# A two-layer diffusion trunk: layer 0's experts in 12 groups instead of 13, gathered and scattered two groups at a time, its branch after the first group, and a ring of 12 weight places

## The chip, the cores and the metric

The kernel runs on one core of one Trainium2 chip, as one program. The metric is the device time of one execution in microseconds. Of the kernel before there are three runs, with a median of 1575.86 us (1575.17 to 1578.94). One more execution was taken with the hardware profiler; every row quoted below comes from that one.

## The reference

256 latent tokens and 256 context tokens of width 1024 go through two layers. A layer is a mixer (layer 0: convolution and differential attention; layer 1: gated linear attention) and then a mixture of 32 experts, of which every token picks two inside one group of eight. Layer 0's experts see all 512 tokens, layer 1's only the 256 latent ones. All weights are 32-bit floats.

```python
def hier_moe(xt, rg_w, rg_b, re_w, re_b, w1, w3, w2):
    lg = (xt @ rg_w).astype(jnp.float32) + rg_b
    pg = jax.nn.softmax(lg, axis=-1)
    _, gi = lax.top_k(lg, 1)
    ...
    top_v, top_i = lax.top_k(le_sel, TOP_K)
    gate = pg_sel * jax.nn.softmax(top_v, axis=-1)
    expert = gi * EXPERTS_PER_GROUP + top_i
    ...
    def expert_block(args):
        xb, e = args
        h = jax.nn.silu(xb @ w1[e]) * (xb @ w3[e])
        return h @ w2[e]
    y_rows = lax.map(expert_block, (x_rows, blk_exp)).reshape(n_row, d)
    y = jax.ops.segment_sum(y_rows * row_gate[:, None].astype(y_rows.dtype), row_tok,
                            num_segments=n_tok + 1)
    return y[:n_tok]
```

W1 and W3 of an expert are 1024 x 512, W2 is 512 x 1024, so that an expert has 6 MB of weights and a layer 192 MB. On the inputs that the reference draws, the experts 0 to 3 of layer 0 get 24, 22, 15 and 17 tokens, the largest of the others 67, and no expert of layer 1 more than 28 (counted by computing the routing of the reference).

## The kernel before

**Weights.** All large weights are read as tiles of 128 x 2048 floats (1024 KB each), issued by SyncE (SP), into a ring of places. An expert is six such tiles, two each of W1, W3 and W2; a layer's experts are 192. Four places are a tile pool with four rotating buffers that lives for the whole kernel (`wt`); others are opened per layer where memory is free by then (`wx`, and in layer 1 a few that reuse other buffers, such as `H`). `wtile` walks round the ring with the counter `ring_at`. In layer 0 the ring has 14 places: four of the base, nine by `LATE`, one by `more`. SP issues in program order, and a load whose place isn't free holds up every later one.

**Groups.** The tokens of an expert are placed in slots, and a group of experts has 128 slots: `PAIR` is two experts with 64 slots each, `MIX` three with 64, 32 and 32, `QUAD` four with 32. Layer 0 has 13 groups, (PAIR, PAIR, (96, 32), MIX, PAIR, MIX, ...), layer 1 has eight QUADs. The first four experts (`E0`) are taken as they are, the others sorted on the chip by their counts, so that full experts meet wide slots; SP then has to read the sorted expert numbers (`numi`, line 1494) into registers before it can issue their loads.

**What a group does.** `group_hot` makes the one-hot matrix P, tokens by slots. `gather` multiplies it with the modulated tokens X, held in two parts XH + XL for precision: 16 matmuls of 128 x 512 (line 1386) put the slots' rows into PSUM, ScalarE and VectorE copy them, and eight transposes (line 1400) turn them into `xgT`. `gates` (line 1431) and `slots_T` (line 1411) make the gates `gc` and the transposed P, `G`. `up` (line 1526) multiplies with W1 and W3, `act_h` makes the gated h and transposes it (line 1443), `down` (line 1535) multiplies with W2, `split_y` splits the result in two parts. `scatter` (line 1463) multiplies with G and adds to the residual H: per 128 tokens two PSUM banks with two matmuls each, then a multiplication on VectorE (line 1467) and an addition, half of it on VectorE and half on GpSimd (line 1468). The gather of the next group and the scatter of the last stand between up and down of the present one.

**The branch.** Tokens that find no slot are handled by `rest`: every engine reads a count (`nri`) and branches over a loop that takes one expert per turn, with six tiles of the ring. In layer 0 it stands after group 3 (`REST`), behind a `scatter` of that group. The loop's six tiles count in `ring_at` although no turn runs: 102 + 271 + 11 loads of expert tiles are in the profile, which is 2 x 192.

**Before the experts.** Layer 0's routing is a long chain on VectorE. `modulate` makes XL for 128 tokens at a time (line 1230), alternately on GpSimd and VectorE; `crowded` sorts the experts. The first 14 tiles are loaded ahead of the routing's end.

## Time and profile before

| what | us |
| --- | --- |
| median of three runs | 1575.86 |
| profiled execution | 1574.82 |
| its span in the trace | 1573.1 |
| PE busy in the span | 1331.3 |
| VectorE busy | 674.0 |
| layer 0's experts, first up matmul to last down matmul | 354.79 to 859.66 |
| layer 0's last addition to H ends | 875.66 |

The profile lists, for every engine, when it was busy and what ended the idle time before an instruction. PE is TensorE, PEld its loading of stationary operands, DVE VectorE, ACT ScalarE, POOL GpSimd, SP SyncE; an engine's name with a q behind it is the engine's instruction stream (issues, branches). A 32-bit float matmul is recorded twice. "DMA share" is the busy share of the core's 16 DMA engines, and GB/s what they moved; "PEclk" is the granted TensorE clock as a share of full speed. L12 is line 12 of the kernel.

### The profile page before, as it was taken

The page shows a single profiled execution, that of the slowest core. Times are in us where ns is not written, and L with a number is a line of the kernel's source. Part 1 is how long each engine was busy: PE and PEld are TensorE (multiplying, and loading weights), DVE is VectorE, ACT ScalarE, POOL GpSimd, SP SyncE. Part 2 cuts the span into 40 slices and gives each one's busy share as a digit, 9 for nine tenths or more (in the row PEclk, how much of TensorE's full clock was granted, in tenths as well). Part 3 has the DMA queues.
Part 4 walks back from the last instruction along what each step waited for, and adds up shares of the span by engine and source line. Part 5 has one row for each costly group of instructions (what it writes and reads, how often), then busy time and mean ns, then how long its engine had stood idle before and what let it go on. Part 6 is the DMA issues. An engine that isn't in the chain of part 4 may idle for free. (4 is left out here: it accounts for less than half of the span.)

```text
span 1573.1 us, 19365 instructions
## 1 busy us (share of the span) xinstructions
PE 1331.3 (85%) x7541; PEld 671.3 (43%) x7541; DVE 674.0 (43%) x1301; ACT 369.0 (23%) x706; POOL 338.7 (22%) x234
## 2 busy tenths in 40 slices
PE   5998989859997999999998799988776678778776
PEld 4765647643443434343332487776322122212211
DVE  4589885762245133334334838676202012102121
ACT  3255554531010100001001366444100000000000
POOL 1477402430012011111012545462000000000000
PEclk9999978889997999999999799999798899999998
DMA  9867162377995799999998824468599999999995
GB/s 315 297 222 256 53 215 58 102 299 295 400 376 213 324 422 423 422 423 422 422 404 293 319 88 161 164 216 321 236 426 426 427 427 427 427 427 426 427 427 240
DMA packets 100829, 498.11 MB, mean 317 GB/s; under 512 B 17605, under 2 KB 30248, under 8 KB 45948
## 3 DMA queue, kind: packets, MB, share of 16 engines
q1 hardware_dynamic: 96780, 490.37, 77.9%
q0 software_dynamic: 1680, 6.16, 1.2%
q8 instruction: 61, 1.00, 0.2%
q10 hardware_dynamic: 2272, 0.28, 0.1%
q14 instruction: 36, 0.29, 0.1%
HBM read 495.68 MB, written 1.10 MB: 316 GB/s over the span
## 5 line engine op out<-in xcount | busy, mean ns | idle before, releaser
L1526 PE MATMUL pj<-wx,xgT 128*32 128x512 f32 (+1 forms) x1616 | 330.9, 639 | 59.7 <-DMA wx<-in_moe_w_dram 56.7
L1468 POOL TENSOR_TENSOR H<-H,sc 128x512 f32<-128x512 f32 x68 | 86.7, 1275 | 899.1 <-DVE sc L1467 899.1
L1535 PE MATMUL pj<-wx,hT 128*32 128x512 f32 (+1 forms) x824 | 184.7, 608 | 5.0 <-ACT hT L1445 2.8
L1440 DVE SCALAR_TENSOR_TENSOR s<-s,gc,pj 128x512 f32<-128x512 f32 x21 | 15.7, 747 | 399.6 <-PE pj L1526 328.4
L1526 PEld LDWEIGHTS pj<-wx,xgT 128*32 128x32 f32 (+1 forms) x1616 | 79.8, 120 | 249.0 <-issue 137.8
L1526 PE MATMUL pj<-wt,xgT 128*32 128x512 f32 (+1 forms) x648 | 151.5, 603 | 18.4 <-DMA wt<-in_moe_w_dram 17.7
L370 POOL TENSOR_TENSOR wl<-wt,wh 128x1024 fp32r<-128x1024 f32 x50 | 126.8, 2543 | 144.0 <-ACT wh L369 135.4
L289 PE MATMUL pj<-wh,XH 128*128 128x512 f32 x304 | 123.7, 418 | 15.2 <-ACT p L621 6.8
L290 PE MATMUL pj<-wl,XH 128*128 128x512 f32 x304 | 124.2, 409 | 1.6 <-POOL wl L370 1.6
L1467 DVE TENSOR_TENSOR sc<-wk,g 128x512 f32<-128x512 f32 x136 | 87.6, 686 | 85.5 <-PE wk L1463 83.7
L291 PE MATMUL pj<-wh,XL 128*128 128x512 f32 x304 | 123.6, 408 | 0.2
L1535 PEld LDWEIGHTS pj<-wx,hT 128*32 128x32 f32 (+1 forms) x824 | 44.1, 115 | 94.1 <-issue 81.6
L369 ACT ACTIVATE wh<-wt 128x1024 fp32r<-128x1024 f32 x66 | 69.3, 1056 | 54.4 <-PE pj L291 35.4
L1468 DVE TENSOR_TENSOR H<-H,sc 128x512 f32<-128x512 f32 x68 | 79.6, 1171 | 2.0
L289 PEld LDWEIGHTS pj<-wh,XH 128*128 128x128 f32 x304 | 59.0, 195 | 44.1 <-issue 10.1
L1526 PEld LDWEIGHTS pj<-wt,xgT 128*32 128x32 f32 (+1 forms) x648 | 38.6, 117 | 90.4 <-issue 56.9
L1439 ACT ACTIVATE s<-pj 128x512 f32<-128x512 f32 x21 | 12.5, 597 | 252.4 <-PE pj L1526 245.2
L543 DVE SCALAR_TENSOR_TENSOR wk<-hp,vt,wk 128x512 f32<-128x512 f32 x90 | 67.6, 751 | 1.7
L290 PEld LDWEIGHTS pj<-wl,XH 128*128 128x128 f32 x304 | 59.4, 195 | 16.4 <-POOL wl L370 2.7
L291 PEld LDWEIGHTS pj<-wh,XL 128*128 128x128 f32 x304 | 59.3, 195 | 15.4 <-DVE XL L1094 1.2
L1535 PE MATMUL pj<-wt,hT 128*32 128x512 f32 (+1 forms) x280 | 62.0, 599 | 2.4 <-ACT hT L1445 2.4
L1445 ACT ACTIVATE hT<-trps 128x512 f32<-128x512 f32 x21 | 12.5, 597 | 215.2 <-PE trps L1443 215.2
(461 smaller groups left out, 1982.0 us busy)
## 6 DMA issues: line engine op xcount, KB each, us to landing
wx<-in_moe_w_dram SPq DMA_DIRECT2D x271, 1024.0 KB, 18.6
wt<-in_moe_w_dram SPq DMA_DIRECT2D x102, 1024.0 KB, 19.4
wa<-in_ada_w_dram SPq DMA_DIRECT2D x16, 1024.0 KB, 5.7
wt<-in_gla_w_in_dram SPq DMA_DIRECT2D x12, 1024.0 KB, 6.9
H<-in_moe_w_dram SPq DMA_DIRECT2D x11, 1024.0 KB, 19.6
S<-in_ada_w_dram SPq DMA_DIRECT2D x10, 1024.0 KB, 5.2
wt<-in_ada_w_dram SPq DMA_DIRECT2D x8, 1024.0 KB, 5.3
wt<-in_ab_w_in_dram SPq DMA_DIRECT2D x6, 1024.0 KB, 10.7
```

The costliest lines, as they stand in the source:

```text
L289: nc.tensor.matmul(ps, sh, mh, start=k0, stop=False)
L290: nc.tensor.matmul(ps, sh, ml, start=False, stop=False)
L291: nc.tensor.matmul(ps, sl, mh, start=False, stop=k1)
L369: nc.scalar.activation(wh, w, AF.Copy)
L370: (nc.vector if dve or alt and q % 2 else nc.gpsimd).tensor_sub(wl, w, wh.bitcast(FT))
L543: e.scalar_tensor_tensor(av, hp[:, cb, :, t:t + 256], cw[:, t, cb:cb + 1], av, op0=OP.mult, op1=OP.add)
L1439: nc.scalar.activation(s, h1, AF.Silu)
L1440: nc.vector.scalar_tensor_tensor(s, s, gc, h3, op0=OP.mult, op1=OP.mult)
L1467: nc.vector.tensor_mul(t, ps[:, c], g2[:, b // 2, c])
L1468: (nc.vector if hf else nc.gpsimd).tensor_add(H[:, b, c], H[:, b, c], t)
L1526: nc.tensor.matmul(ps[o:o + w], xgT[:, k, o:o + w], W[nm, x, k // 4][:, k % 4], start=k == 0, stop=k == 7)
L1535: nc.tensor.matmul(ys[hf][o:o + w], hT[:, k, o:o + w], W["2", x, k // 2][:, k % 2, hf * 512:(hf + 1) * 512], start=k == 0, stop=k == 3)
```

## The change

Layer 0 has 12 groups: the first four experts are one QUAD, and (96, 32), MIX, PAIR, MIX, ... follow. They are handled in pairs, (0, 1), (2, 3) to (10, 11). Layer 1 keeps its groups and its functions.

- `gather0` takes the place of `gather` in layer 0. The tokens X are now the stationary operand and P, 256 slots wide for both groups of a pair, is the moving one; the product is `xgT` itself, so that there are no transposes, and ScalarE copies it out of PSUM. It takes 64 matmuls, 256 columns wide for a pair and 128 wide for the groups 0 and 1, which are gathered singly.
- `scatter0` sums both groups of a pair in one PSUM bank (four matmuls), so that the multiplication and the additions on VectorE and GpSimd run once for two groups. It stands after the up of the next pair's first group.
- `rest` comes after the down of group 0, without a scatter ahead of it, and sets `ring_at` back behind it. Group 1's one-hot matrix, gather and gates come behind `rest`.
- The ring has 12 places (`LATE` 7 for 9), and its four base places have tags of their own instead of a rotating pool; the mixers use them too, so that some loads there take another place.
- `crowded` comes before the first gather; XL is made on GpSimd alone; the loads of a group are asked for at other steps (`i in (2, 4)`).

On the TensorE at layer 0's branch, the program of before ended the pre-branch part with group 3's scatter; these are the last rows ahead of the branch and the branch itself:

```order
L1463 MATMUL wk<-yh,G 128x512 x2
L1463 MATMUL wk<-yl,G 128x512 x2
L1680 TENSOR_LOAD nri
L1681 COMPARE_AND_BRANCH
L1682 TENSOR_LOAD nri
L1683 COMPARE_AND_BRANCH
```

In the changed program the rows at that place are group 0's up, the transposes of h, and its down:

```order
L1547 MATMUL pj<-wx,xgT 32x512 x24
L1547 MATMUL pj<-wt,xgT 32x512 x16
L1450 MATMUL trps<-cst,s 128x128 x4
L1556 MATMUL pj<-wx,hT 32x512 x32
L1701 TENSOR_LOAD nri
L1703 COMPARE_AND_BRANCH
```

The scatter left this place: group 0's part of it now runs with group 1's, inside and behind group 2's up, and the branch is three groups earlier.

On SP's queue, the last rows ahead of the branch before the change are loads for group 4, each behind a wait (ISA) for its place:

```order
L1483 DMA wt<-in_moe_w_dram 128x2048
L1483 ISA
L1483 DMA wx<-in_moe_w_dram 128x2048
L1483 ISA
L1483 DMA wx<-in_moe_w_dram 128x2048
L1681 COMPARE_AND_BRANCH
```

In the changed program the last four loads ahead of the branch are group 1's W1, in the base places; behind them SP reads nine expert numbers and then branches. The rows from the last two of these loads on:

```order
L1503 DMA wt<-in_moe_w_dram 128x2048
L1503 ISA
L1503 DMA wt<-in_moe_w_dram 128x2048
L1514 TENSOR_LOAD numi
L1514 ISA x2
```

So 28 tiles are issued ahead of the branch, of which group 0 uses 24; group 1's other eight come right behind it.

On the TensorE inside a pair, around a group's down, before:

```order
L1535 MATMUL pj<-wx,hT 32x512 x17
L1400 MATMUL trps<-cst,xg 128x128 x4
L1431 MATMUL trps<-tab,P 128x2 x4
L1463 MATMUL wk<-yh,G 128x512 x2
L1463 MATMUL wk<-yl,G 128x512 x2
L1535 MATMUL pj<-wx,hT 32x512 x12
L1411 MATMUL trps<-identr,P 128x128 x4
```

The changed program around the down of group 3 (wt, hT), ahead of which the second half of the next pair's gather (L1382) has just ended:

```order
L1438 MATMUL trps<-tab,P 128x3 x3
L1484 MATMUL wk<-yha,G 128x512
L1484 MATMUL wk<-yla,G 128x512
L1417 MATMUL trps<-identr,P 128x128 x4
L1556 MATMUL pj<-wt,hT 64x512 x8
L1484 MATMUL wk<-yhb,G 128x512
L1484 MATMUL wk<-ylb,G 128x512
```

The transposes of L1400 are gone, and the scatter of a pair opens its banks with the first group's parts (yha, yla), while the second group's (yhb, ylb) follow behind its down.

The diff, cut to its core:

```diff
-TURN = (120, 1)
-LATE = (9, 11)
+LATE = (7, 11)
...
-GROUPS = ((PAIR, PAIR, (96, 32), MIX, PAIR, MIX, PAIR, MIX, PAIR, MIX, PAIR, MIX, MIX), (QUAD,) * 8)
-REST = (3, 1)
+GROUPS = ((QUAD, (96, 32), MIX, PAIR, MIX, PAIR, MIX, PAIR, MIX, PAIR, MIX, MIX), (QUAD,) * 8)
+REST = (0, 1)
...
         if not late:
-            return ring.tile([128, 2048], FT, name="wt", tag="wt")
-        f = late[(ring_at[0] + TURN[1] * (ring_of[1] == "ring0" and ring_at[0] >= TURN[0])) % len(late)]
+            base_at[0] += 1
+            return base(base_at[0] - 1)
         ring_at[0] += 1
-        return f()
+        return late[(ring_at[0] - 1) % len(late)]()
+
+    def base(i):
+        return ring.tile([128, 2048], FT, name="wt", tag=f"wt{i % RING}")
...
-            (nc.gpsimd if last and b % 2 == 0 else nc.vector).tensor_sub(X[1][:, :, t], xv, X[0][:, :, t].bitcast(FT))
+            (nc.gpsimd if last else nc.vector).tensor_sub(X[1][:, :, t], xv, X[0][:, :, t].bitcast(FT))
...
+                def gather0(P, dst):
+                    n = P.shape[-1]
+                    m = min(8, 512 // n)
+                    for k0 in range(0, 8, m):
+                        ps = wk()[:, 0:m * n].rearrange("p (k s) -> p k s", k=m)
+                        for k in range(m):
+                            for b in range(nb):
+                                for h in range(2):
+                                    nc.tensor.matmul(ps[:, k], M['X'][h][:, k0 + k, b * 128:(b + 1) * 128], P[:, b],
+                                                     start=b == 0 and h == 0, stop=b == nb - 1 and h == 1)
+                        nc.scalar.activation(dst[:, k0:k0 + m], ps, AF.Copy)
...
+                def scatter0(Gs, ys):
+                    for b in range(nb):
+                        for hf in range(2):
+                            ps = wk()
+                            n = 2 * len(Gs)
+                            for i in range(n):
+                                nc.tensor.matmul(ps, Gs[i // 2][:, b * 128:(b + 1) * 128], ys[i // 2][i % 2][:, hf], start=i == 0, stop=i == n - 1)
+                            c = slice(512 * hf, 512 * hf + 512)
+                            t = ep.tile([128, 512], FT, name="sc", tag="sc", bufs=2)
+                            nc.vector.tensor_mul(t, ps, g2[:, b // 2, c])
+                            (nc.vector if hf else nc.gpsimd).tensor_add(H[:, b, c], H[:, b, c], t)
...
                     for i, _ in enumerate(zip(*es_)):
-                        if i in (0, 4):
+                        if i in (2, 4):
                             yield W
...
                     n = nc.values_load(nri[0:1, 0:1], min_val=0, max_val=64)
+                    at = ring_at[0]
                     with tc.If(n > 0):
...
+                    if l == 0:
+                        ring_at[0] = at
...
-                    if j == REST[l] and l == 0:
-                        scatter(*prev)
-                        prev = None
-                        rest()
...
+                    for j in range(0, NG, 2):
+                        ys = []
+                        nxt = None
+                        for i in range(2):
+                            g = groups[j + i]
+                            hs = up(W, xgT[:, :, ab[i]], g)
+                            for _ in ld:
+                                pass
+                            hT = act_h(hs[0], hs[1], gc[i])
+                            W2 = W
+                            if i == 0 and prev is not None:
+                                scatter0(*prev)
+                            if j + i + 1 < NG:
+                                ld = load_group(groups[j + i + 1])
+                            if i and j + 2 < NG:
+                                P = frtile([nb, 256], "P", 1)
+                                for x in range(2):
+                                    group_hot(groups[j + 2 + x], P=P[:, :, ab[x]])
+                                nxt = pair_tiles()
+                                gather0(P, nxt[0])
+                                gcn = [prep0(x, groups[j + 2 + x], nxt[1]) for x in range(2)]
+                            y = down(W2, hT, g)
+                            ys.append(split_y(y, "ab"[i]))
+                            if j + i + 1 < NG:
+                                W = next(ld)
+                                if j + i == REST[l]:
+                                    rest()
+                                    P = frtile([nb, 256], "P", 1)
+                                    group_hot(groups[1], P=P[:, :, ab[1]])
+                                    gather0(P[:, :, ab[1]], xgT[:, :, ab[1]])
+                                    gc[1] = prep0(1, groups[1], G)
+                                W = next(ld)
+                        prev = ([G[:, x] for x in range(2)], ys)
+                        if nxt:
+                            (xgT, G), gc = nxt, gcn
+                    scatter0(*prev)
```

More of the change, by code (lines that the diff above doesn't have):

```diff
@@ L113, in wtile @@
         if not late:
-            return ring.tile([128, 2048], FT, name="wt", tag="wt")
-        f = late[(ring_at[0] + TURN[1] * (ring_of[1] == "ring0" and ring_at[0] >= TURN[0])) % len(late)]
+            base_at[0] += 1
+            return base(base_at[0] - 1)
         ring_at[0] += 1
-        return f()
+        return late[(ring_at[0] - 1) % len(late)]()
+    def base(i):
+        return ring.tile([128, 2048], FT, name="wt", tag=f"wt{i % RING}")
     def open_ring(es, name, side, n, more=(), order=None):
-        f = [lambda: ring.tile([128, 2048], FT, name="wt", tag="wt")] * RING
+        f = [lambda i=i: base(i) for i in range(base_at[0], base_at[0] + RING)]
         for i in range(n):
@@ L1726, in moe, with pair_tiles, prep0 @@
-                scatter(*prev)
+                            if l:
+                                scatter(pre[1], split_y(ov_down(W, hT2)))
+                            else:
+                                scatter0([pre[1]], [split_y(ov_down(W, hT2), "b")])
+                    if l == 0:
+                        ring_at[0] = at
+                NG = len(groups)
+                if l == 0:
+                    P = frtile([nb, 256], "P", 1)
+                    ab = [slice(0, 128), slice(128, 256)]
+                    def pair_tiles():
+                        return (ep.tile([128, 8, 256], FT, name="xgT", tag="xgT", bufs=1),
+                                frtile([2, nb * 128], "G", 2))
+                    def prep0(i, g, G):
+                        gc = gates(P[:, :, ab[i]], g)
+                        slots_T(P[:, :, ab[i]], G=G[:, i])
+                        return gc
+                    group_hot(groups[0], pos0, P[:, :, ab[0]])
+                    crowded()
+                    xgT, G = pair_tiles()
+                    gather0(P[:, :, ab[0]], xgT[:, :, ab[0]])
+                    gc = [prep0(0, groups[0], G), None]
+                    prev = None
+                    ld = load_group(groups[0])
+                    for _ in range(2):
+                        W = next(ld)
[26 more added lines that the diff above has]
+                                    rest()
+                                    P = frtile([nb, 256], "P", 1)
+                                    group_hot(groups[1], P=P[:, :, ab[1]])
+                                    gather0(P[:, :, ab[1]], xgT[:, :, ab[1]])
+                                    gc[1] = prep0(1, groups[1], G)
+                                W = next(ld)
+                        prev = ([G[:, x] for x in range(2)], ys)
+                        if nxt:
+                            (xgT, G), gc = nxt, gcn
+                    scatter0(*prev)
+                else:
+                    P0 = group_hot(groups[0], pos0)
+                    crowded()
+                    pr = prep(groups[0], P0)
+                    nG = slots_T(pr[1])
+                    prev = None
+                    ld = load_group(groups[0])
+                    for _ in range(2):
+                        W = next(ld)
+                    for j, g in enumerate(groups):
+                        xgT, P, gc = pr
+                        G = nG
+                        hs = up(W, xgT, g)
+                        for _ in ld:
+                            pass
+                        hT = act_h(hs[0], hs[1], gc)
+                        W2 = W
+                        if j + 1 < NG:
+                            ld = load_group(groups[j + 1])
+                        if j + 1 < NG:
+                            pr = prep(groups[j + 1], group_hot(groups[j + 1]))
+                        if prev is not None:
+                            scatter(*prev)
+                        if j + 1 < NG:
+                            nG = slots_T(pr[1])
+                        if j == REST[l]:
+                            rest()
+                        ys = down(W2, hT, g)
+                        if j + 1 < NG:
+                            for _ in range(2):
+                                W = next(ld)
+                        prev = (G, split_y(ys))
+                    scatter(*prev)
```

85 lines of the change are left out of this document (24 added, 61 removed).

## The prediction

> **What bounds the kernel now.** I read the page's slices first, then a table of windows over layer 0's experts, then the timeline around the place where the table shows a hole. In the page's slices (DMA's busy tenths, and what the DMA engines moved; a slice is 39 us) both expert stages stand out at 422 to 427 GB/s, with one low slice in the first of them, the thirteenth:
>
> ```profile
> DMA  9867162377995799999998824468599999999995
> GB/s 315 297 222 256 53 215 58 102 299 295 400 376 213 324 422 423 422 423 422 422 404 293 319 88 161 164 216 321 236 426 426 427 427 427 427 427 426 427 427 240
> ```
>
> The windows (PE, PEld, DVE, ACT and POOL busy with counts, then granted clock, DMA share, GB/s) show the stage itself and its losses:
>
> ```profile
> 350.00:360.00 10.00, 8.63 (x40) 4.10 (x39) 0.69 (x1) 1.19 (x2) 0.00 (x0) 0.97 0.07 14
> 360.00:370.00 10.00, 10.00 (x51) 4.17 (x50) 1.29 (x4) 1.88 (x2) 0.00 (x0) 1.00 0.99 397
> 380.00:390.00 10.00, 10.00 (x47) 3.61 (x48) 2.01 (x3) 2.39 (x4) 0.00 (x0) 1.00 0.63 238
> 450.00:460.00 10.00, 10.00 (x83) 3.42 (x85) 6.03 (x9) 0.00 (x0) 2.57 (x2) 1.00 0.83 321
> 480.00:490.00 10.00, 9.70 (x68) 4.23 (x60) 3.77 (x7) 0.00 (x0) 1.28 (x1) 1.00 1.02 427
> 490.00:500.00 10.00, 5.20 (x12) 2.86 (x12) 8.55 (x12) 1.57 (x3) 3.81 (x3) 0.70 0.16 67
> 500.00:510.00 10.00, 6.23 (x12) 3.50 (x12) 7.12 (x9) 0.00 (x0) 3.81 (x3) 0.50 0.01 2
> 510.00:520.00 10.00, 7.07 (x22) 2.44 (x24) 3.38 (x6) 0.00 (x0) 1.27 (x1) 0.61 0.03 5
> 520.00:530.00 10.00, 10.00 (x47) 3.80 (x44) 0.57 (x1) 0.60 (x1) 0.00 (x0) 1.00 0.99 397
> 560.00:800.00 240.00, 227.72 (x1200) 92.82 (x1204) 84.64 (x133) 23.14 (x42) 30.64 (x24) 1.00 1.01 419
> ```
>
> From 560 to 800 us the DMA engines are never free (share 1.01): the weights bound the stage, and a tile of 1024 KB (1.0486 MB) costs 1.0486 / 419 = **2.503 us**. From 490 to 520 the share is 0.16, 0.01 and 0.03, which is 28 us of nothing (30 x 0.933). PE is 95% busy in the bound stretch, so it is close behind.
>
> The timeline around the hole, and SP's waits from 460 to 522 us:
>
> ```profile
> 472.91 47.00 SPq L1483 DMA_DIRECT2D wx<-in_moe_w_dram  x4
> 507.85 1.22 PE L1463 MATMUL wk<-yh,G 128*128 128x512 f32 x2 [1.45 <-DVE sc L1467]
> 511.36 1.26 DVE L1468 TENSOR_TENSOR H<-H,sc 128x512 f32<-128x512 f32 x1
> 512.93 6.06 PE L1526 MATMUL pj<-wx,xgT 128*64 128x512 f32 x16 [3.00 <-DVEq L1681]
> 512.95 0.83 DVE L1512 TENSOR_TENSOR P<-cst,tab 128x256 fp32r<-128x256 f32 x3 [0.33 <-DVEq L1681]
> ...
> SPq L1483 <- PE pj L1526: 38.3, 4, 30.3
> ```
>
> SP isn't held by the branch: it waits 30.3 us in one piece for a place, until the up of group 4 has used its first tile at 519 us. Eight tiles were in store for group 4, and six places of the 14 were counted for the loop that no turn of ran. Meanwhile PE does group 3's scatter, each of whose steps waits 1.45 us for VectorE, at half the clock, and then the branch. So the hole is two things: no place, and work between the last down and the next up.
>
> **The frame.** The first three of these rows give the stage's ends, the last two its last scatter step:
>
> ```profile
> 354.79 3.65 PE L1526 MATMUL pj<-wt,xgT 128*64 128x512 f32 x16 [0.69 <-ACT xgT L1406]
> 358.46 0.80 SPq L1481 DMA_DIRECT2D wt<-in_moe_w_dram  x2
> 856.00 3.66 PE L1535 MATMUL pj<-wt,hT 128*32 128x512 f32 x32
> 873.07 1.29 DVE L1467 TENSOR_TENSOR sc<-wk,g 128x512 f32<-128x512 f32 x2 [0.94 <-PE wk L1463]
> 874.39 1.27 DVE L1468 TENSOR_TENSOR H<-H,sc 128x512 f32<-128x512 f32 x1
> ```
>
> First up to last down is 859.66 - 354.79 = 504.9 us, and the scatter behind it 875.66 - 859.66 = 16.0. I count from the profiled execution, 1574.82 (span 1573.1 and 1.7 around it); the median of the three runs lies 1.0 above it, and I add that at the end.
>
> **First up of the changed kernel, t0.** What ends the chain to it today:
>
> ```profile
> 338.70 2.85 POOL L1230 TENSOR_TENSOR XL<-x,XH 128x1024 fp32r<-128x1024 f32 x1
> 340.88 2.44 DVE L1230 TENSOR_TENSOR XL<-x,XH 128x1024 fp32r<-128x1024 f32 x1 [2.02 <-ACT XH L1229]
> 346.46 0.74 DVE L1512 TENSOR_TENSOR P<-cst,pj 128x256 fp32r<-128x256 f32 x2
> 347.26 0.79 PE L1386 MATMUL wk<-XH,P 128*128 128x512 f32 x1 [7.77 <-DVE P L1512]
> ```
>
> The XL of 2.44 us leaves VectorE's chain; a QUAD needs four comparisons instead of two (0.37 each: +0.7), so P is there 1.7 us sooner, at 345.5. GpSimd makes both, 2.85 each from 338.70 on: ready at 344.4, in time. From 347.26 to 354.79 there were 7.5 us of gather, copy, transposes, copy. The new gather is 64 matmuls. Their price isn't in the trace with 128 columns and X standing; the nearest rows are a product in the mixer of layer 1 with 128 x 128 weights and 256 columns, of which thirteen follow one another between these two:
>
> ```profile
> 893.79 0.28 PE L868 MATMUL pj<-XH,wh 128*128 128x256 f32 x1
> 895.16 0.28 PE L868 MATMUL pj<-XL,wh 128*128 128x256 f32 x1
> 655.61 0.54 PE L1411 MATMUL trps<-identr,P 128*128 128x128 f32 x4
> ```
>
> (895.16 - 893.79) / 12 = 0.114 us each; the four 128-column transposes take 0.54 together, 0.46 to the next start, again 0.115 each. So 128 columns aren't cheaper than 256: 64 x 0.115 = 7.4, with the first 16 at half clock 9, and 0.6 to copy; crowded's transposes and their copies stand inside it, 0.5. That is 345.5 + 10.1 = 355.6, **+0.8**. In mixer 0 two tiles of the modulation weights now stand two tiles ahead of two others; if what they displace is waited for, that is two tiles of 2.5 us: 0 to 5, I take +2.5. So t0 = **358.1** (bounds 354.5 to 362).
>
> **The stage.** 12 tiles are in store at t0 (14 before), 180 follow. The first place comes free 3.7 us after t0 (358.46 - 354.79), the first bytes 1.9 later (397 of 419 GB/s in 360 to 370 says they flow from about 360.4). Then 180 x 2.503 = 450.5, and the last half of a down, 3.7. That is 459.8 if nothing tears the stream.
>
> *At the branch.* Group 0's tiles 13 to 24 land until t0 + 5.6 + 30 = t0 + 35.6, its down ends at t0 + 39.3, split_y (ScalarE, then VectorE with the row below) about t0 + 42, and engines leave the branch 0.33 us after VectorE's last work (row 512.95). Tiles 25 to 28, asked for before it, keep the DMA engines busy until t0 + 45.6. After the branch eight places are free at once, since all of group 0 is used and `ring_at` is set back: the hole is **0 to 2 us**. That a branch needn't tear the stream is seen in layer 1, whose branch stands behind an up, with loads in flight:
>
> ```profile
> 1190.00:1200.00 10.00, 6.10 (x32) 2.26 (x35) 5.62 (x14) 0.38 (x1) 2.52 (x2) 0.68 1.01 422
> 1195.46 1.03 PE L1535 MATMUL pj<-H,hT 128*32 128x512 f32 x1 [3.00 <-DVEq L1681]
> ```
>
> The same 3.00 us wait, and a DMA share of 1.01. PE then gathers group 1 (9 to 10 us) and starts its up at about t0 + 53; the 12 places are full at t0 + 65.6, nine us after the first of them is used.
>
> *PE behind the DMA.* The rows for a group at full clock (the last is VectorE's part of split_y):
>
> ```profile
> 630.88 0.50 PE L1386 MATMUL wk<-XH,P 128*128 128x512 f32 x1
> 634.81 7.49 PE L1526 MATMUL pj<-wx,xgT 128*32 128x512 f32 x66
> 646.31 0.75 PE L1443 MATMUL trps<-cst,s 128*128 128x128 f32 x4 [0.99 <-DVE s L1440]
> 650.14 0.95 PE L1431 MATMUL trps<-tab,P 128*128 128x2 f32 x8
> 657.91 0.73 PE L1463 MATMUL wk<-yh,G 128*128 128x512 f32 x2
> 658.48 0.63 PE L1463 MATMUL wk<-yl,G 128*128 128x512 f32 x2
> 470.05 1.28 DVE L1453 TENSOR_TENSOR yl<-pj,yh 128x512 fp32r<-128x512 f32 x2
> ```
>
> Up is 128 records of 0.113 = 14.4, down 64 of 0.114 = 7.3, small transposes and gates 2.2. Before, gather (16 matmuls from 630.88 to 634.81, 3.9), its eight transposes (some 1.3 by the rows of four) and scatter (4 x 1.2 = 4.8) make 33.9 a group, 67.8 for two. Now two groups share 64 x 0.115 = 7.4 of gather and 32 x 0.28 = 9 of scatter: 47.8 + 16.4 = **64.2** against 67.8. Two groups of MIX and PAIR are 30 tiles, 75 us. So PE has 11 us of slack per pair, and VectorE and GpSimd do half the scatter passes. The longest stretch of PE in which no place comes free is a scatter by VectorE's pace, 4 x 2.6 = 10, with transposes; the ring holds 12 x 2.5 = 30. Before, register reads and PE's lag cost 3.7 us in 380 to 390 and 1.7 in 450 to 460, some 7 in all from 360 to 470; the register reads stay, the two PAIRs in front, where PE lags most, go. I take **3** (0 to 8).
>
> Stage: 459.8 + 1 + 3 = **463.8**, that is 41.1 less than 504.9.
>
> **The tail.** The last scatter takes two groups at once: VectorE's two multiplications and one addition are 2.6 us per 128 tokens, 10.4, with split_y and a step at either end 13.5, **-2.5** (0 if PE runs at half clock: eight matmuls of 0.5 are 4 x 4 = 16). Layer 1 is the same work in nearly the same order: I take 0, -1 to +2.
>
> **The sum.** t0 + 3.3, stage - 41.1, tail - 2.5: -40.3. 1574.82 - 40.3 + 1.0 = **1535.5**.
>
> **The rivals.**
> *The hole only moves.* If the loads behind the branch had to wait for group 1's up, as today's wait for group 4's, the stream would stop from t0 + 45.6 to t0 + 53 + 3.7 + 1.9 = t0 + 58.6, 13 us: **1548**. For it: that is just what SP's row of 30.3 us shows. Against it: no place is left uncounted, and group 0 is used up. 0.15.
> *The ring is too short.* Two places fewer, and gathers in one piece: if each of the five borders between pairs starves the stream of 5 us, as 380 to 390 nearly did, +25: **1560**. Against it: 30 us of store over stretches of 10 to 13. 0.09.
> *The clock.* PE idles more, a sixth of each pair, and if the granted clock falls as in the scatter of 490 to 510 (0.50), PE becomes the bound. At a clock of 64.2 / 75 = 0.86 it catches the DMA engines; the gain of 40 us over five and a half pairs, 7.3 each, is lost at 82 us a pair, a clock of 0.78; at 0.74 it is 87 us, +66 - 40: **1600**, the slower side. Against it: 1.00 in all of 560 to 800. By the Trainium skill, "TensorE: Matmul & The Clock Gate", Part 1: The HAM clock gate, the array falls to half clock after an idle window of about 3.4 us and needs as long a busy one to come back. The trace falls to 0.50 with idle pieces of only 1.45 us, so it is harsher than the rule there; by the rule only the waits for DMA at a pair's end would count, one of about 11 us, and one slow window after it is hidden in the same slack. 0.05.
> *It doesn't do what it says:* a loop turn would run if one of the experts 0 to 3 had over 32 tokens; they have 24, 22, 15 and 17, so it can't on these inputs. *Something unforeseen takes the gain* (about 1575): 0.05.
>
> **How the numbers follow.** Forecast 0.66, with its own range 1524 to 1545 from the bounds of t0, losses and tail; the rivals as above. 8 in 10 needs the forecast's range and the first rival's, with a few us on either side for its own bounds: **1522 to 1557**. A measurement of this kernel can tell about 0.3%, 4.7 us: faster 0.90 (forecast and the first two rivals), same 0.04 (most of the unforeseen), slower 0.06.
>
> **What would show it.** Right: a DMA share of 0.9 and more in each 10 us behind t0 + 6, the branch's included; SP's longest wait for a place well under 30 us; PE's clock 1.00; 0.115 us per matmul of the new gather. Wrong: a window under 0.3 near t0 + 46 to 60 (the first rival); shares of 0.6 to 0.9 at each pair (the second); a clock under 0.9 (the third); t0 above 362 (mixer 0).

## The result, and the profile after

| | median, us | runs | span of the profiled execution |
| --- | --- | --- | --- |
| before | 1575.51 | 1575.12 to 1578.94 | 1573.1 |
| after | 1548.99 | 1548.82 to 1549.05 | 1547.1 |

The ratio is 0.983, with an interval from 0.981 to 0.9844: 26.5 us gained where 40 were forecast, 13.5 us above the forecast of 1535.5. Layer 0's last addition to H shows the same difference: it ends at 848.9 us, 26.8 sooner than before; the rest of the kernel is as long as it was (698.2 us behind it, 697.4 before). All of gain and loss therefore lies in layer 0's experts and ahead of them.

In the page of after, the busy tenths of DMA and the GB/s moved, a slice being 38.7 us:

```profile
DMA  9857262164989999999999534568799999999996
GB/s 318 294 202 258 90 218 59 55 254 196 411 327 423 423 419 422 423 424 422 423 423 401 207 116 141 181 204 338 287 426 426 426 427 427 426 427 427 427 427 253
```

The low slice of before (213 GB/s, the thirteenth) is gone. Two smaller dents stand in its place, 196 in the tenth slice and 327 in the twelfth. The windows of after say what they are (PE, PEld, DVE, ACT and POOL busy with counts, granted clock, DMA share, GB/s):

```profile
350.00:360.00 10.00, 9.75 (x46) 9.75 (x47) 3.11 (x31) 0.60 (x1) 0.85 (x2) 0.50 0.30 109
360.00:370.00 10.00, 10.00 (x50) 6.22 (x52) 1.05 (x4) 0.60 (x1) 0.00 (x0) 0.57 0.00 0
370.00:380.00 10.00, 10.00 (x94) 3.73 (x88) 2.34 (x9) 2.48 (x3) 0.00 (x0) 1.00 0.75 296
410.00:420.00 10.00, 6.90 (x33) 6.93 (x33) 1.04 (x4) 0.00 (x0) 0.00 (x0) 0.65 0.95 378
420.00:430.00 10.00, 10.00 (x53) 9.23 (x56) 1.25 (x7) 1.79 (x3) 0.00 (x0) 0.50 1.01 424
430.00:440.00 10.00, 10.00 (x84) 2.73 (x80) 0.72 (x3) 0.60 (x1) 0.00 (x0) 0.82 0.79 305
450.00:460.00 10.00, 10.00 (x81) 6.87 (x84) 0.91 (x6) 2.17 (x5) 0.00 (x0) 1.00 0.64 268
460.00:470.00 10.00, 10.00 (x96) 2.99 (x92) 2.75 (x7) 1.66 (x3) 0.00 (x0) 1.00 0.82 320
560.00:800.00 240.00, 220.67 (x1364) 95.18 (x1356) 47.36 (x84) 26.42 (x45) 15.40 (x12) 1.00 1.01 422
```

At the branch (410 to 430) the weights flow on, as forecast. They stand still from 360 to 370, and after the branch, from 430 to 470, they lose (1 - 0.79) + (1 - 0.64) + (1 - 0.82) of 10 us each, 7.5 us. Ahead of both places TensorE runs at a clock of 0.50. The timeline of after, at the first gather, at the branch and at the end of the layer:

```profile
344.53 0.29 DVE L1306 TENSOR_TENSOR Aa<-pj,bo 128x128 bf16<-128x128 f32 x1
349.32 0.87 DVE L1533 TENSOR_TENSOR P<-cst,pj 128x128 fp32r<-128x128 f32 x4
350.25 0.47 PE L1382 MATMUL wk<-P,XH 128*128 128x128 f32 x1 [3.92 <-DVE P L1533]
350.52 0.41 PE L1382 MATMUL wk<-P,XL 128*128 128x128 f32 x1
...
364.84 0.41 PE L1382 MATMUL wk<-P,XL 128*128 128x128 f32 x1
365.18 3.62 PE L1547 MATMUL pj<-wt,xgT 128*32 128x512 f32 x10
371.43 2.18 SPq L1501 DMA_DIRECT2D wt<-in_moe_w_dram  x4
...
405.24 3.62 PE L1556 MATMUL pj<-wx,hT 128*32 128x512 f32 x20 [0.69 <-SPq L1703]
413.10 0.45 PE L1382 MATMUL wk<-P,XH 128*128 128x128 f32 x1 [4.24 <-DVE P L1533]
426.57 0.41 PE L1382 MATMUL wk<-P,XL 128*128 128x128 f32 x1
429.11 3.64 PE L1547 MATMUL pj<-wt,xgT 128*32 128x512 f32 x16
...
847.61 1.27 DVE L1488 TENSOR_TENSOR H<-H,sc 128x512 f32<-128x512 f32 x1
```

The 64 products of the first gather take 14.9 us up to the first up, the second single gather 13.7 from its first product to the start of the matmul behind its last; before, gather, copies and transposes took 7.5 (347.26 to 354.79). The first up of after starts at 365.2, 10.4 us later than before, and the first reload 6.25 us behind it (3.7 before).

Now TensorE's own time, from the up behind the branch to the last down: 346.8 us and nine groups before, 408.4 us and eleven groups after. The rows give PE busy, then clock, DMA share and GB/s, and behind them PE's two largest waits and those for the weights. Before:

```profile
512.90:859.70 346.80, 328.96 (x1797) 0.99 0.98 402
...
PE trps L1443 <- DVE s L1440: 7.6, 8, 1.0
PE wk L1463 <- DVE sc L1467: 3.8, 6, 1.5
...
PE pj L1526 <- DMA wx<-in_moe_w_dram: 1.6, 2, 1.4
```

After:

```profile
429.10:837.50 408.40, 376.59 (x2378) 0.99 0.99 413
...
PE pj L1547 <- DMA wx<-in_moe_w_dram: 11.4, 9, 1.5
PE trps L1450 <- DVE s L1447: 4.7, 5, 0.9
PE pj L1547 <- DMA wt<-in_moe_w_dram: 4.4, 4, 1.4
...
PE pj L1556 <- DMA wx<-in_moe_w_dram: 2.8, 3, 1.6
```

Before, TensorE waited 1.6 us for weights in 347: whatever the DMA share says, the weights did not hold it up. Its own time, everything but waits for weights, was (346.8 - 1.6) / 9 = 38.4 us a group. After, it waits 11.4 + 4.4 + 2.8 = 18.6 us for weights, and its own time is (408.4 - 18.6) / 11 = **35.4** a group, where the weights ask for 168 tiles x 2.503 / 11 = 38.2.

### The profile page after: what moved, and what is told of

It is laid out like the page before. It is cut to its first block, busy times and chain, and to the rows that moved or that the text cites. A ratio compares the mean times of both kernels' runs of the same rounds, so it can differ in the third digit from the quotient of the medians.

```text
span 1547.1 us, 19403 instructions
## 1 busy us (share of the span) xinstructions
PE 1297.3 (84%) x7645; PEld 674.8 (44%) x7645; DVE 585.5 (38%) x1187; ACT 366.9 (24%) x699; POOL 304.5 (20%) x207
## 3 DMA queue, kind: packets, MB, share of 16 engines
q8 instruction: 62, 1.02, 0.3%
## 5 line engine op out<-in xcount | busy, mean ns | idle before, releaser
L1547 PE MATMUL pj<-wx,xgT 128*32 128x512 f32 (+1 forms) x1528 | 306.2, 634 | 64.1 <-DMA wx<-in_moe_w_dram 64.1
L1547 PE MATMUL pj<-wt,xgT 128*32 128x512 f32 (+1 forms) x736 | 167.1, 645 | 26.3 <-DMA wt<-in_moe_w_dram 26.3
L1547 PEld LDWEIGHTS pj<-wx,xgT 128*32 128x32 f32 (+1 forms) x1528 | 72.6, 118 | 257.5 <-issue 129.9
L1447 DVE SCALAR_TENSOR_TENSOR s<-s,gc,pj 128x512 f32<-128x512 f32 x20 | 14.9, 747 | 434.3 <-PE pj L1547 373.1
L1556 PE MATMUL pj<-wx,hT 128*32 128x512 f32 (+1 forms) x808 | 165.0, 606 | 11.4 <-DMA wx<-in_moe_w_dram 6.0
L291 PE MATMUL pj<-wh,XH 128*128 128x512 f32 x304 | 123.9, 418 | 18.8 <-ACT p L623 10.1
L1488 POOL TENSOR_TENSOR H<-H,sc 128x512 f32<-128x512 f32 x24 | 30.8, 1283 | 397.5 <-DVE sc L1487 396.2
L1475 POOL TENSOR_TENSOR H<-H,sc 128x512 f32<-128x512 f32 x16 | 20.4, 1274 | 444.5 <-DVE sc L1474 444.5
L1556 PEld LDWEIGHTS pj<-wx,hT 128*32 128x32 f32 (+1 forms) x808 | 40.6, 114 | 93.6 <-issue 67.1
L291 PEld LDWEIGHTS pj<-wh,XH 128*128 128x128 f32 x304 | 58.9, 195 | 48.8 <-ACT p L623 11.4
L1382 PE MATMUL wk<-P,XH 128*128 128x256 f32 (+1 forms) x224 | 67.0, 327 | 11.2 <-DVE P L1533 8.2
L1382 PE MATMUL wk<-P,XL 128*128 128x256 f32 (+1 forms) x224 | 66.0, 322 | 0.0
```

Of the source, the lines that this page charges most:

```text
L291: nc.tensor.matmul(ps, sh, mh, start=k0, stop=False)
L1382: nc.tensor.matmul(ps[:, k], M['X'][h][:, k0 + k, b * 128:(b + 1) * 128], P[:, b], start=b == 0 and h == 0, stop=b == nb - 1 and h == 1)
L1447: nc.vector.scalar_tensor_tensor(s, s, gc, h3, op0=OP.mult, op1=OP.mult)
L1475: (nc.vector if hf else nc.gpsimd).tensor_add(H[:, b, c], H[:, b, c], t)
L1488: (nc.vector if hf else nc.gpsimd).tensor_add(H[:, b, c], H[:, b, c], t)
L1547: nc.tensor.matmul(ps[o:o + w], xgT[:, k, o:o + w], W[nm, x, k // 4][:, k % 4], start=k == 0, stop=k == 7)
```

## The experiments

Eleven of the twelve kernels came of three questions: what bounded the kernel before, where the 13.5 us went, and what the pairing is worth; the twelfth tried for more. In the texts of the expectations M stands for the theory that mixer 0 runs later because the base places have tags of their own, C1 and C2 for two readings of the slow first gather, D for the weights and P for TensorE's queue as the bound before, R for missing places at the branch, Q for TensorE's time per pair, V for VectorE's passes. "First up" is layer 0's first up matmul, "H ends" the last addition to H in layer 0, "rest" the span behind it. e_warm and e_idle add matmuls whose results nobody reads. The kernel before, run beside each of them, had medians of 1573.5 to 1575.0, so medians of different kernels compare to some 2 us; "rest" differs more than that, so effects on layer 0 are read from "H ends".

| kernel | median, us | ratio to before, interval | first up | H ends | rest |
| --- | --- | --- | --- | --- | --- |
| b_reset | 1574.95 | 1.0003 (0.9993 to 1.0012) | 353.8 | 878.1 | 693.8 |
| b_12 | 1555.33 | 0.9877 (0.9855 to 0.9899) | 354.3 | 854.5 | 699.2 |
| b_12_reset | 1544.6 | 0.9816 (0.9796 to 0.9835) | 354.9 | 850.4 | 692.4 |
| e_noreset | 1562.68 | 0.9923 (0.9906 to 0.994) | 368.5 | 859.1 | 702.2 |
| e_rot | 1546.14 | 0.982 (0.9803 to 0.9836) | 359.5 | 843.5 | 701.7 |
| e_oldg | 1545.12 | 0.9808 (0.9789 to 0.9827) | 362.6 | 841.1 | 704.1 |
| e_warm | 1546.76 | 0.9824 (0.9808 to 0.984) | 365.7 | 842.2 | 703.5 |
| e_rot_oldg | 1532.77 | 0.9731 (0.9713 to 0.9749) | 354.4 | 830.8 | 700.4 |
| e_idle | 1532.62 | 0.9741 (0.9721 to 0.9761) | 352.8 | 830.3 | 697.1 |
| e_ungath | 1541.28 | 0.9791 (0.9775 to 0.9808) | 354.2 | 838.7 | 696.9 |
| e_unscat | 1534.1 | 0.9748 (0.9731 to 0.9764) | 354.5 | 831.0 | 699.7 |
| e_unpair | 1554.2 | 0.987 (0.9847 to 0.9894) | 353.8 | 850.7 | 700.3 |

**b_reset: the kernel before, with the counter set back behind `rest`.** This is meant to close the part of the hole that missing places make.

```diff
+                    at = ring_at[0]
                     with tc.If(n > 0):
...
+                    if l == 0:
+                        ring_at[0] = at
```

> The kernel before with one edit: ring_at is set back behind the branch of layer 0, so that no place stays uncounted for the loop. Theory R (the 28 us without transfers are mostly missing places): six more tiles, 15 us, are asked for at once; the hole shrinks to about 13 us; time about 1561. Rival (the hole is group 3's scatter, its half clock and the branch, places or not): SP still waits for the up of group 4, hole over 24 us, time over 1571.

Nothing was gained, though the hole did end sooner. The windows of b_reset (the row at 510 had a share of 0.03 and 5 GB/s before):

```profile
510.00:520.00 10.00, 8.01 (x28) 2.74 (x30) 2.47 (x5) 0.00 (x0) 1.13 (x1) 0.66 0.99 389
560.00:800.00 240.00, 230.15 (x1201) 93.36 (x1205) 84.96 (x133) 24.17 (x43) 30.63 (x24) 1.00 0.98 403
```

Some 10 us more of weights were moved at 510, and the share from 560 to 800 fell from 1.01 to 0.98: the weights now wait for places. From 490 to 510 the hole stands as before (shares 0.07 and 0.01), so that about 10 of its 28 us were closed; SP's longest wait there, 21.3 us, is now put down to TensorE's branch. TensorE has no wait for weights in layer 0's experts in it; before, it had 1.6 us in all, and more than that the hole can't have cost. So the hole, in which the forecast saw 28 us, cost next to nothing by itself: the weights made it up while TensorE was busy. H even ends 2.4 us later: the downs (L1535) take 135.4 us of TensorE where they took 128.1, with the same matmuls in another order.

**b_12 and b_12_reset: the kernel before with the 12 groups of the change and the branch after the third, without and with the counter set back.**

```diff
-GROUPS = ((PAIR, PAIR, (96, 32), MIX, PAIR, MIX, PAIR, MIX, PAIR, MIX, PAIR, MIX, MIX), (QUAD,) * 8)
-REST = (3, 1)
+GROUPS = ((QUAD, (96, 32), MIX, PAIR, MIX, PAIR, MIX, PAIR, MIX, PAIR, MIX, MIX), (QUAD,) * 8)
+REST = (2, 1)
```

> The kernel before with the 12 groups of the change (QUAD first) and its branch after group 2, which is after the same 54 tiles as before; gather, scatter, ring of 14 and the uncounted six places as before. Theory P (before, TensorE's queue bounds layer 0's experts: 38.5 us per group from group 4 on, with 1.6 us of waits for DMA in all; the hole in the transfers lies beside it): one group of TensorE less, but now the transfers with their hole bound: 3.7 + 1.9 + 178 x 2.503 + 28 + 7 + 3.7 = 490 us against 504.9, time about 1560. Rival D (the transfers bound before the change): one group less on TensorE changes nothing, time 1572 to 1578.

> As b_12, and ring_at set back behind the branch. Theory P: with TensorE no longer the bound, the places now matter, unlike in b_reset: the hole is 9 to 15 us shorter than in b_12 and so is the time: 1545 to 1551. Rival (the hole's length never matters): the time of b_12.

The same weights with one group less end layer 0's experts 21.1 us sooner (875.7 to 854.5), although the hole still stands there. That is the opposite of what a stage bound by weights does. It isn't what theory P forecast either, that the weights and their hole bound now: TensorE waits for weights 1.4 us in all of b_12's stage, and not at all in b_12_reset's. One group less does not bring the full 38.4 us of a group; the downs, for one, take 138.5 us where they took 128.1. The counter then brings 10.7 us of the median, of which only 4.2 are in layer 0 (854.5 to 850.4), about what the downs give back (134.9 after 138.5); the other 6.8 are in the rest, about which more below. So that b_12_reset came out at the foot of its range, 1545 to 1551, doesn't bear out the reason given for it. The window at the branch in b_12, and the same in b_12_reset:

```profile
480.00:490.00 10.00, 5.54 (x14) 2.59 (x15) 6.69 (x10) 0.00 (x0) 2.74 (x3) 0.50 0.01 4
```

```profile
480.00:490.00 10.00, 5.31 (x12) 2.91 (x14) 7.38 (x11) 0.00 (x0) 3.46 (x3) 0.50 0.34 114
```

**e_noreset: the change without the counter set back.**

```diff
-                    if l == 0:
-                        ring_at[0] = at
```

> The changed kernel without setting ring_at back: six of the 12 places stay uncounted at the branch. Theory P (the changed kernel is bound by its transfers): two loads instead of eight can start behind the branch, the stream stops for 10 to 15 us until group 1's up: time 1558 to 1564. Rival (TensorE still bounds there, and the places are as idle as in b_reset): within 3 us of the changed kernel.

By the median it is 13.7 us slower than after, within the range of theory P, but only about half of that lies where the edit acts. Between the first up and H's end it takes 6.8 us more (490.5 against 483.7); 3.3 us stand ahead of the first up, where the source is the same, and 4.0 in the rest. Here the hole appears, behind the branch, as the prediction's first rival had it:

```profile
420.00:430.00 10.00, 10.00 (x49) 10.00 (x48) 0.00 (x0) 1.19 (x2) 0.00 (x0) 0.50 0.15 64
430.00:440.00 10.00, 10.00 (x76) 3.54 (x80) 1.97 (x8) 0.60 (x1) 0.00 (x0) 0.76 0.23 76
```

SP's third load behind the branch waits until group 1's up has begun (436.66, the up 431.27). The two windows lose 16 us of weights, where the dents of after lose 7.5. The same edit is worth nothing in layer 0 of the kernel before and some 7 us in the changed one, where TensorE runs ahead of the weights and waits for them.

**e_rot: the change, with the four base places one rotating pool again.**

```diff
-    ring = ctx.enter_context(tc.tile_pool(name="ring", bufs=1))
+    ring = ctx.enter_context(tc.tile_pool(name="ring", bufs=RING))
-        return ring.tile([128, 2048], FT, name="wt", tag=f"wt{i % RING}")
+        return ring.tile([128, 2048], FT, name="wt", tag="wt")
```

> The changed kernel with the four base places as one rotating pool again, as before the change; all else as changed. Theory M (the tags of their own reorder loads in mixer 0 and cost it 6.0 us: VectorE's Aa at 344.53 instead of 338.56): Aa near 338.6, time about 1543. Rival (the 6 us come from elsewhere in the program, or are hidden behind the first loads anyway): Aa near 344.5, or time within 2 us of 1549.

VectorE's step `Aa`, at 344.53 in after, first in before and then in e_rot:

```profile
338.56 0.29 DVE L1304 TENSOR_TENSOR Aa<-pj,bo 128x128 bf16<-128x128 f32 x1
```

```profile
338.78 0.29 DVE L1306 TENSOR_TENSOR Aa<-pj,bo 128x128 bf16<-128x128 f32 x1
```

So 5.75 of the 6.0 us of mixer 0 come of the tags, the only edit. They come in two steps: SP's loads in after stand 2.6 us behind those of e_rot at 84 us (83.94 against 81.34) and 5.75 at 317 (316.82 against 311.07). The size isn't fixed: `Aa` lies between 344.5 and 347.9 in the kernels with the tags. H ends 5.4 us sooner than in after, but the median fell by only 2.9, since the rest took 3.5 more.

**e_oldg: the change, with the groups 0 and 1, the two single gathers, in the form of before** (`gather1`, P standing and X moving, with copies and transposes; the pairs keep `gather0`).

```diff
-                    gather0(P[:, :, ab[0]], xgT[:, :, ab[0]])
+                    gather1(P[:, :, ab[0]], xgT[:, :, ab[0]])
-                                    gather0(P[:, :, ab[1]], xgT[:, :, ab[1]])
+                                    gather1(P[:, :, ab[1]], xgT[:, :, ab[1]])
```

> The changed kernel with groups 0 and 1, which are gathered singly, in the form of before (P standing, 16 matmuls of 512 columns, eight transposes); pairs keep the new form. Theory C (the 64 products with 128 columns run wholly at half clock, 0.213 us each, and so cost 6 to 7 us at the first up and again at the up behind the branch, where the stream of weights then lacks places): first up 7 us earlier, near 358; group 1's up 5 to 6 us earlier after its branch; time 1536 to 1540. Rival (the losses behind the branch come from the ring of 12 and the branch's own wait, not from the gather): only the first up's 7 us: about 1542.

From P's start to the first up 11.05 us, against 15.9 in after; mixer 0 came out 2.3 us later still (`Aa` at 346.8), and yet H ends 7.8 sooner. The DMA share is 0.94 or more from 370 on, but for one window of 0.78: the dent behind the branch goes with the slow second gather. The median, 1545.1, lies above both expectations: mixer 0 took back 2.3 us and the rest 5.9.

**e_warm: the change, with 12 unread matmuls of 128 x 512 ahead of each single gather.**

```diff
+                            for _ in range(n):
+                                nc.tensor.matmul(wm, P[:, 0], M['X'][0][:, 0:4, 0:128], start=True, stop=True)
```

> The changed kernel with 12 extra matmuls of 512 columns (their output is read by nobody) between P and the gather, for groups 0 and 1. They cost some 4.4 us each time (8 at half clock, 4 at full). Theory C1 (the clock rises under wide products and stays up in the narrow ones): 0.115 us per narrow product, first up 1 to 2 us earlier than in the changed kernel; time 1546 to 1549. Rival C2 (products of 128 columns with a new stationary operand each can't hold the clock up): they fall back to 0.213 after some us; first up 1 to 4 us later, time 1551 to 1557.

The timeline of e_warm:

```profile
351.67 5.49 PE L1739 MATMUL wk<-XH,P 128*128 128x512 f32 x12 [3.93 <-DVE P L1533]
...
365.45 0.27 PE L1382 MATMUL wk<-P,XL 128*128 128x128 f32 x1
365.65 3.62 PE L1547 MATMUL pj<-wt,xgT 128*32 128x512 f32 x26
```

The window from 360 to 370 has a clock of 1.00 where after has 0.57. The wide matmuls take 5.5 us and the 64 products then 8.7 instead of 14.9, so that the first gather gains next to nothing; the first up runs at full speed, the first reload comes 3.65 us after it instead of 6.25, and H ends 6.7 us sooner. So C1 holds for the clock, though not for the first up, which it had 1 to 2 us earlier. The narrow products are slow because of the clock: behind the branch of e_warm all 64 follow one another at 0.11 us, close to the forecast's 0.115. They hold a clock that has risen; by themselves they did not raise it in after, in 14.9 us and in 13.5.

**e_rot_oldg: both of these together.**

> The changed kernel with both: base places as one rotating pool, and groups 0 and 1 gathered in the form of before. If the two gains add: Aa near 338.7, first up near 354.6, layer 0's end some 14 us before the changed kernel's. The end of the program has followed only in part so far (layer 1's first up ran at half clock in e_rot and e_oldg and at full clock in the changed kernel): time 1534 to 1542. Rival (something later takes whatever layer 0 gains): 1545.

1532.77, 16.2 us below after and the fastest of the kernels that the study had until then. Alone the two edits are worth 5.4 and 7.8 us of layer 0, together 18.1. It is the forecast's kernel in all but the form of two gathers: first up at 354.4, DMA 1.01 to 1.02 behind the branch (420 to 440: 422 and 427 GB/s), and 2.7 us off 1535.5. Of what the sum of the two lacks, 2.3 us are mixer 0 in e_oldg.

**e_unpair, e_ungath, e_unscat: e_rot_oldg with pairs taken apart, gather and scatter both, gather alone, scatter alone.** All three start their first up at about the same time, so the stretch behind the branch can be compared.

```diff
-                                scatter0(*prev)
+                                for x in range(2):
+                                    scatter0(prev[0][x:x + 1], prev[1][x:x + 1])
...
-                                gather0(P, nxt[0])
+                                for x in range(2):
+                                    gather1(P[:, :, ab[x]], nxt[0][:, :, ab[x]])
```

> e_rot_oldg without the pairing: every group gathered in the form of before (16 matmuls of 512 columns, eight transposes, into its half of xgT) and scattered by itself (two matmuls per bank, VectorE's and GpSimd's pass per group). Theory Q (pairing is what keeps TensorE below the transfers): TensorE needs 38.5 us per group as before, 77 per pair against 75 of transfers, and the last scatter 16 us instead of 11: time 1540 to 1548. Rival (12 groups alone keep it below; pairing is hidden but for the tail): 1533 to 1538.

> This is e_rot_oldg (the change with one rotating pool of base places and the first two groups gathered in the old form), 1532.77 us, with the pairing of the gather alone taken back: each later group gathers by its own selection products, scatters stay in pairs. Both kernels compute the reference. Theory Q (TensorE's own time per pair decides, and the gather's form is where the pairing saves it): a pair's gather and its transposes cost 2 x (3.8 + 1.3) = 10.2 us unpaired against 7.4 paired, 2.8 us on five pairs, 14 us: 1544 to 1550, most of the 21 us that e_unpair lost. Rival V (the scatter's form decides, through VectorE's passes over the result and the cuts they make between down products): 1531 to 1537 here.

> e_rot_oldg with the pairing of the scatter alone taken back: each pair's two groups are scattered one after the other at the same place, gathers stay in pairs. Theory Q: the scatters' products are nearly as long in all (a matmul of 64 rows takes as long as one of 128, so 2 x 4.8 against some 5.6 us a pair, but the downs of the next group stand ready and the weights run beside them), most of it seen at the end of the layer, where one more scatter and its pass over the result stand alone, 4 to 5 us: 1536 to 1541. Rival V: 1545 to 1553, most of the 21 us of e_unpair.

From 0.8 to 1.3 us into the up behind the branch to the last down (span, then PE busy, clock, DMA share, GB/s), in the order e_rot_oldg, e_unscat, e_ungath, e_unpair:

```profile
409.80:819.40 409.60, 383.43 (x2377) 0.98 1.01 420
```

```profile
409.80:819.60 409.80, 387.06 (x2389) 0.99 1.01 420
```

```profile
409.50:827.30 417.80, 394.86 (x2297) 1.00 0.99 411
```

```profile
409.50:839.40 429.90, 407.18 (x2305) 1.00 0.97 400
```

PE's waits for weights in these stretches are 11.9, 7.6, 8.7 and 5.2 us. Its own time is what is left: 397.7, 402.2, 409.1 and 424.7. The stretch stays at 409.7 as long as TensorE's own time is below about 402 (the weights set it, share 1.01), and grows with it beyond. So the scatter's pairing alone is worth 1.3 us of the median (0.2 of H's end), the gather's 8.5 (7.9), and both 21.4 (19.9): the first few us of TensorE are free, the later ones count. Against Q's ranges e_ungath lies 3 us low, e_unscat 2 us low and e_unpair 6 us high; the sum of the two was to be the whole, and isn't. V falls as it was put, but the scatter's form isn't free: behind unpaired gathers it is worth 12.9 us of the median. By line, the scatter's matmuls take 8.1 us more in e_unscat than in e_rot_oldg (55.7 against 47.6), and the downs 5.2 less (88.4 against 93.5), which hides most of it; in e_unpair the scatter takes 10.2 more, the downs 2.0 more and the ups 6.6 more. That is part of why both together add 27.0 us to TensorE's own time where each alone adds 4.5 and 11.4; why the matmuls stood in an order that made the ups and downs dearer stays open.

b_12_reset, with 12 groups and no pairing, ends H at 850.4, as e_unpair does (850.7). By the median it is even 4.4 us faster than after, and yet its layer 0 ends 1.5 us later: the rest makes the difference (692.4 against 698.2).

**e_idle: e_rot_oldg with 9 and 7 unread matmuls in TensorE's wait ahead of each layer's first gather.**

> e_rot_oldg with a few extra matmuls of 512 columns (9 in layer 0, 7 in layer 1, output read by nobody) in TensorE's wait ahead of the first gather of each layer's experts, on a copy of the positions so that they can't start earlier. Theory C (the first gather and up of a layer run at half clock because of that wait, and wide products raise the clock): the gather of 16 matmuls takes 4 to 5 us instead of 6.5 and layer 1's first up 3.6 us instead of 5.3; time 1526 to 1530. Rival (the clock's window decides, a few us of work don't): 1532 to 1535.

In its profiled execution the first gather took 4.8 us, and layer 0's first up stood 1.6 sooner, but H ended only 0.4 sooner. Layer 1's first up ran at full clock there, as theory C had it (3.63 us for 30 records, 5.33 in e_rot_oldg), and the rest took 3.3 us less; but that execution, 1529.2, was the fastest of five that reach to 1535.8, and the median is the same. As a way to gain it is a miss.

## Why the prediction came out as it did

- **"The weights bound the stage"** was the step that failed. It was read off a DMA share of 1.01, which says that transfers are in flight, not that anyone waits for them; PE's waits for weights, 1.6 us in 347, say it. b_reset shows it by closing a third of the hole for nothing, b_12 by gaining 21.1 us with the hole in it. The forecast's time is added up from the changed kernel's own weights, tile by tile, so that this error did not enter the sum.
- **The number** owes something to luck. 1549 lies above the forecast's own range of 1524 to 1545, and within 1522 to 1557 only because that left room for the first rival, whose hole did not come.
- **PE per group**, put at 33.9, is where this went wrong. Measured over nine groups it is 36.6 us busy and 38.4 with waits for other engines. Most of the difference is the down, put at 7.3 by the row of an undivided one; in that stretch it is 95.95 / 9 = 10.7 (the rows of the downs alone, L1535 before and L1556 after):

```profile
512.90:859.70 346.80, 95.95 (x448) 24.43 (x448) 0.99 0.98 402
...
429.10:837.50 408.40, 94.09 (x576) 26.67 (x576) 0.99 0.99 413
```

  The timeline of before has the likely reason in its pieces:

```profile
576.91 1.91 PE L1535 MATMUL pj<-wt,hT 128*32 128x512 f32 x8
...
659.04 1.90 PE L1535 MATMUL pj<-wx,hT 128*32 128x512 f32 x4
```

  In after, a whole down undivided, of a MIX, whose 64 slots run as two pieces of 32 columns beside the other two:

```profile
566.87 7.10 PE L1556 MATMUL pj<-wx,hT 128*32 128x512 f32 x64 [0.75 <-ACT hT L1452]
```

  A piece of four records takes as long as one of eight, 1.9 us, that is 0.475 a record against 0.111 in the undivided one. We read it so: the slots of a group stand in different columns of the array and run side by side, which a piece cut off by transposes or scatters does less. The Trainium skill, "TensorE: Matmul & The Clock Gate", Part 3: Packing small matmuls — row/col tiling, says that matmuls in different tiles of the array overlap; the rows agree for a long run and show that short ones lose part of it. After, the downs take 94.09 / 11 = 8.6 a group. That the cuts are the whole difference is read from the rows, and wasn't tried. The changed kernel's 64.2 a pair, 32.1 a group, was low for the same kind of reason: its own time is 35.4, so that the slack is 5.6 us a pair and not 11.
- **The pairing** was costed as 3.6 us of slack per pair that nobody needed. It is what moved the bound from TensorE to the weights: e_unpair gives back 21.4 of e_rot_oldg's 42 us. The forecast had the end state right, with an unbroken stream of weights behind it, and the wrong reason for the gain: one group less and pairs, not the hole.
- **The hole** at the branch doesn't come back, as forecast, and the reset is what prevents it (e_noreset: 6.8 us between the first up and H's end; the first rival's own working, 13). The time came close to that rival's 1548 by another way.
- **First up**, put at +3.3, came at +10.4, at 365.2 and so beyond its bounds of 354.5 to 362; the prediction's own sign for this, t0 above 362, came true. Two terms were mis-sized. Mixer 0, taken as +2.5 out of 0 to 5, was +6.0 (e_rot). The first gather, put at 10.1 us with 16 products at half clock, was 14.9 with all 64 at half clock (0.213 us each). The chain from `Aa` to P shortened by 3.0, more than the 1.7 forecast.
- **The stage**, put at 463.8, was 472.3 (365.18 to 837.46). The second single gather, also at half clock, put the up behind the branch at 64 us after the first up instead of 53, the ring filled, and 7.5 us of DMA were lost from 430 to 470, against losses of 1 + 3; the first reload came 2.6 us later. That the slow gathers cost this is what e_oldg and e_warm show: from 430 to 500 the weights lose 2.2 and 2.6 us in them against 7.0 in after, and from the first up to H's end they take 478.5 and 476.5 us against 483.7, where the forecast had 477.3. For the first reload only e_warm speaks; in e_oldg it comes 6.97 us behind the first up, with transposes and gates between the parts of that up. SP could not have issued it much sooner in after: with a QUAD first, group 1's loads need the sorted expert numbers, and SP began to read them at 369.9, 1.5 us ahead of that reload, which the prediction did not count. Some 2 us remain unassigned.
- **The tail** came out 2 us better than forecast: 11.4 us where 13.5 was put and 16.0 was before. 7.1 + 8.5 - 2.1 is the 13.5 us that were missed. (The profiled executions miss by 14.3: layer 1 took 0.8 more. The median of after lies 0.2 us above its profile, where 1.0 was added.)
- **The clock as a rival** was looked for in the pairs, where it stayed at 1.00 as forecast. It struck where the forecast had given it 1.6 us.

## What to carry to other kernels

To say which of two busy things bounds a stage, look at what the one waits for the other, not at how busy it is: here a DMA share of 1.01 stood beside 1.6 us of waits. Where two bounds lie within a few per cent, an edit that relieves one can measure as nothing and still be worth some 7 us after the other is relieved, so try such edits together as well as singly. After a wait, starting TensorE on wide products paid here with some 7 us of layer 0 (e_oldg, e_warm), though not where wide ones came first already (e_idle); price an operation that starts from idle by rows that did so too, and a divided one by divided rows.

## What the runs showed of the hardware

- Products of 128 x 128 with 128 columns and a new stationary each ran at half clock for 14.9 us in after without a pause over 0.2 us, and did not raise it; after 12 matmuls of 512 columns, in e_warm, the same products held 1.00. Under the wide gather the clock rose after 3.2 us in before (from 0.43 to 0.235 us each at 350.4) and after 5.7 us in e_rot_oldg. The Trainium skill, "TensorE: Matmul & The Clock Gate", Part 1: The HAM clock gate, calls the warm-up a budget of about 3.4 us of time and not a number of matmuls; the wide rows lie between just under that and twice as much, the narrow ones are four times beyond it and don't agree.
- The span behind layer 0 has nearly the same program in all of these kernels, yet took 692 to 704 us. Part of it is layer 1's first up, which runs at half clock in some and not in others: first after, then e_oldg.

```profile
1095.22 3.63 PE L1547 MATMUL pj<-wx,xgT 128*32 128x512 f32 x30
```

```profile
1089.98 6.18 PE L1571 MATMUL pj<-wx,xgT 128*32 128x512 f32 x30
```

  In the five kernels where this up took 3.63 us or so the rest is 692.4 to 698.2 us, in the nine where it took 5.3 to 6.3 it is 697.4 to 704.1 (before and after included). So up to some 3 us of a gain in layer 0 can be lost there. That the moment at which TensorE arrives decides it is a guess, and what makes up the remainder of the twelve was not traced.
